# First layer's shift and scale summed by matmuls in four column groups, and split tiles read back through SyncE's queue

## The chip, the cores and the metric

One core of one Trainium2 chip (trn2). The metric is the device time of one execution in microseconds (us), lower is better. The engines are named as in the profile: PE (TensorE matmuls), PEld (its weight loads), DVE (VectorE), ACT (ScalarE), POOL (GpSimd), SP (SyncE, which here only issues DMAs).

## The reference

Two layers over x of 2048 tokens by 1024 features, one batch. Cut to what matters here:

```python
cond = jax.nn.silu(c)                                # 1024 numbers
for layer in range(2):
    mod = cond @ ada_w[layer] + ada_b[layer]         # 1024 x 3072 matrix, one row times matrix
    shift, scale, gate = jnp.split(mod, 3, axis=-1)
    h = x * (1.0 + scale) + shift
    if layer == 0:
        y = even_mixer(h)   # h @ w_in (1024 x 2816) -> windowed attention, gMLP gating, SiLU gate, @ w_out
    else:
        y = odd_mixer(h)    # h @ w_in (1024 x 2048) -> conv, gates (8 heads of 128 x 128), two scans, @ w_out
    x = layer_norm(alpha * x + gate * y)
```

All is float32. Every large product is made of three matmuls on operands that are split into a high and a low part: a is ahi + alo, b is bhi + blo, and the product is ahi*bhi + ahi*blo + alo*bhi.

## The kernel before

**The start (to about 55 us).** `modulation(...)` is called four times for layer 0, for shift and scale (`part` 0 and 1) of each half `n` of the features. Each call loads two tiles `aw` (1 MB each, [128, 4, 512], L166) through SP into a ring of three, and DVE adds up over the eight slices k in `macc`: L171 multiplies slice 0 by `cond[:, 0]`, L173 multiplies and adds the seven others. The 128 partition rows of `macc` are then summed on PE by four matmuls with a column of ones (L193), which also turn the result into a column, and DVE adds the bias (L198, L200). `build(u)` (L305-327) loads x (`xp`), transposes it on PE (L316), applies scale and shift on ACT (`hm`, L320), splits it into `hhi` and `hlo` (L148 on ACT, L149 on DVE) and stores both to `h_d` in DRAM. `split_w` (L475) loads eight tiles `raw` of the first weights and splits them into `wqh` (ACT, L148) and `wql` (DVE, L149). In code this goes half by half: shift and scale of n, build and split_w of n, then `project(blk)` runs the first products (L152 to L154 with `wqh`, `wql`, `hhi`, `hlo`).

**Even layer.** Attention runs block by block (scores L414, `P` shuffled by DMAs at L450, values L460). `load_hT` (L507-516) then reads `ahi`/`alo` of chunk t back from `h_d` with 8 DMAs on POOL's queue (L512, L513), and 12 to 40 weight units per chunk come as `raw` over SP and are split into the ring `hl` (8 buffers). Beside it, `prepare` splits all weights of the odd layer and stores them to `w_d` (40 tiles) and `wo_d` (16 tiles) of 512 KB.

**Odd layer (from about 890 us).** Four chunks t of 512 tokens and two halves s: `x_job` and `g_job` take 8 `hl` tiles each half and kind, loaded by `unit1` (L866) from `w_d` through POOL's queue; every tile serves 12 matmuls. `front` takes one `hg` tile per group of 128 features (L938, ring of 2) for the gate products `pm`, then ACT and DVE do gates and scans (L976 to L1010), POOL copies carries (L985, L990, L995) and adds the two directions (L996). `back` stores y (L1019, `y_d<-T`) and the carry weights (L1021, `b_d<-ii`) through SP. At the end `unit_out` (L1043) and `resident` (L1060) read `wo_d` on POOL's queue, and the tail reads `y_d` and `b_d` back on SP.

**What sets the order.** A scheduler with a model of the engines puts the instructions of each engine in one list ahead of time; each engine, and each queue of DMA issues, works its list off in that order. An instruction that waits holds up all behind it on its engine. A DMA tile in DRAM is float32; the split tiles in SBUF are float32r, the same 32 bits. Before, POOL's DMAs are given the two types as they stand.

Of the kernel before, what the change touches and what calls it, by code (L numbers as in the profile page):

```python
# [7 lines left out]
F32 = mybir.dt.float32  # L8
F32R = mybir.dt.float32r
I32 = mybir.dt.int32  # L10
AF = mybir.ActivationFunctionType
# [7 lines left out]
KD = D // 128  # L19
# [34 lines left out]
def kernel(  # L54
# [27 lines left out]
    nc = tc.nc  # L82
    act = nc.scalar.activation
# [19 lines left out]
    h_d = []  # L103
# [11 lines left out]
    wo_d = []  # L115
# [3 lines left out]
    w_d = []  # L119
# [8 lines left out]
    cond = const.tile([128, KD], F32, name="cond")  # L128
# [27 lines left out]
    def bank(p, tag, shape=(128, C)):  # L156
        t = p.tile(list(shape), F32, tag=tag, name=tag)
        return t

    def modulation(mp, pp, tag, layer, part, n, gate=None):  # L160
        c0 = part * D + n * C
        acc = mp.tile([128, C], F32, tag="macc", bufs=2, name="macc")
        m = mp.m
        for k2 in range(KD // m):
            aw = mp.tile([128, m, C], F32, tag=tag, name="aw")
            load(out=aw, in_=ada_w[layer, k2 * m * 128:(k2 + 1) * m * 128, c0:c0 + C].rearrange(  # L166
                "(j p) n -> p j n", p=128))
            for j in range(m):
                k = m * k2 + j
                if k == 0:  # L170
                    ts(out=acc, in0=aw[:, j], scalar1=cond[:, 0:1], scalar2=None, op0=ALU.mult)  # L171
                else:
                    stt(out=acc, in0=aw[:, j], scalar=cond[:, k:k + 1], in1=acc, op0=ALU.mult, op1=ALU.add)  # L173
        ps = bank(*pp)
        if part == 2:
            brow = mp.tile([1, C], F32, tag="brow", bufs=1, name="brow")
            load(out=brow, in_=ada_b[layer:layer + 1, c0:c0 + C])
            tt(out=acc[0:1, :], in0=acc[0:1, :], in1=brow, op=ALU.add)
            nc.tensor.matmul(ps, lhsT=ones, rhs=acc, start=True, stop=True)
            act(out=gate[:, n * C:n * C + C], in_=ps, func=AF.Copy)  # L180
            return
        if layer == 0:
            pr, ks = slice(0, 128), slice(4 * n, 4 * n + 4)
            parts = acc.rearrange("p (k m) -> p k m", k=4)
        else:
            pr, ks = slice(64 * n, 64 * n + 64), slice(0, 8)
            parts = mp.tile([128, 8, 64], F32, tag="parts", bufs=1, name="parts")
            for a in range(2):
                nc.vector.tensor_copy(parts[:, :, 32 * a:32 * a + 32],
                                      acc[:, 256 * a:256 * a + 256].rearrange("p (k q) -> p k q", k=8))  # L190
        w = ks.stop - ks.start
        for k in range(w):
            nc.tensor.matmul(ps[pr, k:k + 1], lhsT=parts[:, k], rhs=ones[:, 0:1], start=True, stop=True)  # L193
        dst = (shift, scale)[part][pr, layer, ks]
        v0 = layer * 24 + part * 8
        bias = vcol0[pr, v0 + ks.start:v0 + ks.stop]
        if part == 1:
            stt(out=dst, in0=ps[pr, 0:w], scalar=1.0, in1=bias, op0=ALU.add, op1=ALU.add)  # L198
        else:
            tt(out=dst, in0=ps[pr, 0:w], in1=bias, op=ALU.add)  # L200
# [4 lines left out]
    ap = pool(sb, "attn", right)  # L205
    ss = ExitStack()
    st = pool(ss, "setup", right)
# [26 lines left out]
    ps = bank(px, "px")  # L234
    nc.tensor.transpose(ps[:, 0:8], crow, ident[0:8, 0:8])
    act(out=cond, in_=ps[:, 0:8], func=AF.Silu)

    class Ring:
        def __init__(self, p, q, tag, bufs, m):
# [238 lines left out]
    wqh = jp.tile([128, KD, 768], F32R, name="wqh")  # L478
    wql = jp.tile([128, KD, 768], F32R, name="wql")
    for n in range(2):  # L480
        modulation(Ring(ap, st, "P", 3, 4), (psc, "psc"), "aw", 0, 0, n)
        modulation(Ring(ap, st, "P", 3, 4), (psc, "psc"), "aw", 0, 1, n)
        build(0, range(2 * n, 2 * n + 2))
        split_w(range(4 * n, 4 * n + 4))
        build(1, range(2 * n, 2 * n + 2))
# [22 lines left out]
    def load_hT(t):  # L508
        hT = ([], [])
        for k2 in range(4):  # L510
            hi, lo = act_pair()
            nc.gpsimd.dma_start(out=hi, in_=h_d[t][0][:, 2 * k2:2 * k2 + 2, :])  # L512
            nc.gpsimd.dma_start(out=lo, in_=h_d[t][1][:, 2 * k2:2 * k2 + 2, :])  # L513
            for j in range(2):
                hT[0].append(hi[:, j])
                hT[1].append(lo[:, j])
        return hT
# [345 lines left out]

    def unit1(i):
        hl = cp.tile([128, 2, C], F32R, tag="hl", bufs=8, name="hl")
        nc.gpsimd.dma_start(out=hl, in_=w_d[i])  # L866
        return hl

    def job1(hT, c0):
# [46 lines left out]
    def front(t, s, X):  # L916
# [4 lines left out]
        for g0 in range(0, 4, BATCH):  # L921
# [3 lines left out]
            for i in range(g0, g0 + BATCH):  # L925
# [9 lines left out]
                xlo = el("xlo", 2, F32R)  # L935
                split(xhi[:, w], xlo[:, w], xc[:, w])
                hl = rp.tile([128, 2, C], F32R, tag="hg", bufs=2, name="hg")
                nc.gpsimd.dma_start(out=hl, in_=w_d[32 + g])  # L938
                ra[i] = el2("ra", NEL)
                T[i] = el2("T", NEL)  # L940
                ii[i] = el2("ii", NEL)
# [98 lines left out]

    def unit_out(i):
        hl = cp.tile([128, 2, C], F32R, tag="hl", bufs=8, name="hl")
        nc.gpsimd.dma_start(out=hl, in_=wo_d[i])  # L1043
        return hl

    def part_out(ps, hl, k):
# [10 lines left out]

    def resident(p, n, k):
        w = p.tile([128, 2, C], F32R, name=f"wo{n}_{k}")
        nc.gpsimd.dma_start(out=w, in_=wo_d[n * KD + k])  # L1060
        wo[n][k] = w

    oq = pool(ctx, "outq", left)
# [126 lines left out]
```

## Time and profile before

| | |
|---|---|
| median of 3 runs | 1597.9 us (1594.98, 1597.9, 1599.78) |
| profiled execution, own time | 1601.77 us |
| its span, first to last instruction | 1600.0 us |
| mean granted TensorE clock | 0.977 |
| PE busy | 1481.9 us, 93 % |
| DVE / ACT / POOL busy | 1241.8 / 780.8 / 514.5 us |
| DMA | 366.73 MB, mean 229 GB/s |

The profile is of one execution: busy time is what an engine's instructions took, idle time is put down to what ended it. PE's instructions overlap in the pipeline, so a matmul that lasts 0.39 us lets the next one start after 0.23 us: the step from start to start in a timeline is what one of a row of matmuls costs.

### The profile page before, as it was taken

The numbers are of one execution on the slowest core, as the hardware profiler recorded it, in microseconds if no ns is written. First come the engines' busy times: TensorE is split into PE (matmuls) and PEld (weight loads), VectorE is DVE, ScalarE is ACT, GpSimd is POOL, SyncE is SP. The second block draws the span as 40 slices with busy tenths as digits, with TensorE's granted clock in tenths as the row PEclk, the third lists the DMA queues.
The fourth block names the chain that finished last, engine by engine and source line by source line (L and its number), as shares of the span: only waits on it lengthen the run. The fifth ranks groups of instructions, "written<-read, shape, count | busy, mean of one in ns | idle before, by whom it ended". The sixth has DMA issues, their size and how long they took to land. (4 is left out here: it accounts for less than half of the span.)

```text
span 1600.0 us, 21817 instructions
## 1 busy us (share of the span) xinstructions
PE 1481.9 (93%) x7032; PEld 1189.1 (74%) x7032; DVE 1241.8 (78%) x2243; ACT 780.8 (49%) x1454; POOL 514.5 (32%) x703
## 2 busy tenths in 40 slices
PE   3999999989999999999999879999899899979997
PEld 3887777757788777878877668777777778867886
DVE  8589888754689668857966756989979989887785
ACT  3577777542433432333334128388389588761100
POOL 1023222111004002200211445768657765423121
PEclk9899999999999999999999999999999999989999
DMA  9366776848899898988765698786797677569652
GB/s 341 120 171 202 208 214 190 251 129 293 251 309 278 256 280 290 334 255 266 260 232 165 191 236 212 230 203 223 241 213 225 189 227 234 169 212 367 218 198 85
DMA packets 204603, 366.73 MB, mean 229 GB/s; under 512 B 54568, under 2 KB 100804, under 8 KB 204488
## 3 DMA queue, kind: packets, MB, share of 16 engines
q1 hardware_dynamic: 166632, 235.25, 47.8%
q0 software_dynamic: 37856, 130.08, 26.9%
q8 instruction: 56, 0.92, 0.2%
q14 instruction: 59, 0.48, 0.1%
HBM read 264.07 MB, written 79.68 MB: 215 GB/s over the span
## 5 line engine op out<-in xcount | busy, mean ns | idle before, releaser
L148 ACT ACTIVATE hl<-raw 128x512 fp32r<-128x512 f32 x192 | 118.4, 627 | 197.9 <-DMA raw<-in_ev_w_in_dram 122.3
L152 PE MATMUL pj<-ahi,hl 128*128 128x512 f32 x512 | 201.5, 397 | 11.1 <-DMA hl<-w_d 10.0
L153 PE MATMUL pj<-alo,hl 128*128 128x512 f32 x512 | 201.8, 394 | 0.0
L154 PE MATMUL pj<-ahi,hl 128*128 128x512 f32 x512 | 201.2, 394 | 0.0
L149 DVE TENSOR_TENSOR hl<-raw,hl 128x512 fp32r<-128x512 f32 x192 | 132.1, 697 | 70.4 <-ACT hl L148 70.0
L152 PEld LDWEIGHTS pj<-ahi,hl 128*128 128x128 f32 x512 | 97.4, 190 | 35.3 <-DMA hl<-w_d 12.9
L154 PEld LDWEIGHTS pj<-ahi,hl 128*128 128x128 f32 x512 | 97.3, 190 | 20.9
L153 PEld LDWEIGHTS pj<-alo,hl 128*128 128x128 f32 x512 | 97.5, 190 | 20.4
L866 POOL DMA_DIRECT2D hl<-w_d x128 | 70.6, 554 | 77.8 <-PE pj L154 64.7
L148 ACT ACTIVATE phl<-praw 128x512 fp32r<-128x512 f32 x56 | 35.4, 632 | 122.1 <-DMA praw<-in_od_w_in_dram 63.7
L450 POOL DMA_DIRECT2D P<-T x88 | 49.6, 571 | 135.5 <-DVE T L443 96.5
L512 POOL DMA_DIRECT2D ahi<-h_d x16 | 8.8, 551 | 255.4 <-PE px L154 142.6
L415 DVE CUSTOM_DVE_ANT_0 P<-psc,mask,nsink 128x384 f32<-128x384 f32 (+1 forms) x128 | 73.7, 596 | 20.6 <-PE psc L414 20.0
L154 PE MATMUL pj<-wqh,hlo 128*128 128x512 f32 (+1 forms) x256 | 85.0, 346 | 3.7 <-DVE hlo L149 3.7
L152 PE MATMUL pj<-wqh,hhi 128*128 128x256 f32 (+1 forms) x256 | 88.1, 347 | 0.0
L153 PE MATMUL pj<-wql,hhi 128*128 128x256 f32 (+1 forms) x256 | 87.9, 343 | 0.0
L418 ACT ACTIVATE P<-P,nm 128x384 f32<-128x384 f32 (+1 forms) x128 | 76.8, 604 | 22.6 <-DVE nm L415 20.9
L148 ACT ACTIVATE ahi<-yt 128x512 fp32r<-128x512 f32 (+1 forms) x44 | 32.4, 745 | 107.5 <-DVE yt L1086 68.6
L144 POOL TENSOR_SCALAR rstd<-mv 128x1 f32<-128x1 f32 x32 | 24.5, 764 | 186.9 <-DVE mv L601 163.7
L762 POOL TENSOR_TENSOR alo<-hm,ahi 128x512 fp32r<-128x512 f32 x32 | 47.4, 1486 | 97.4 <-PE pja L154 65.5
L152 PE MATMUL pm<-xhi,hg 128*128 128x512 f32 (+3 forms) x160 | 57.5, 372 | 22.7 <-ACT ra L951 13.9
L932 DVE SCALAR_TENSOR_TENSOR xc<-X,vcol,xc 128x512 f32<-128x512 f32 (+2 forms) x96 | 77.8, 834 | 0.3
(297 smaller groups left out, 4502.9 us busy)
## 6 DMA issues: line engine op xcount, KB each, us to landing
hl<-w_d POOLq DMA_DIRECT2D x128, 512.0 KB, 5.3
raw<-in_ev_w_in_dram SPq DMA_DIRECT2D x128, 256.0 KB, 4.0
w_d<-phl SPq DMA_DIRECT2D x40, 512.0 KB, 4.3
aw<-in_ada_w_dram SPq DMA_DIRECT2D x32, 512.0 KB, 5.9
hg<-w_d POOLq DMA_DIRECT2D x32, 512.0 KB, 4.8
P<-T SPq DMA_DIRECT2D x128, 96.0 KB, 4.1
aw<-in_ada_w_dram SPq DMA_DIRECT2D x8, 1024.0 KB, 8.5
xp<-in_x_dram SPq DMA_DIRECT2D x32, 256.0 KB, 3.5
```

The lines of the kernel that those rows point to most:

```text
L144: nc.gpsimd.tensor_scalar(out=dst, in0=src, scalar1=mul, scalar2=EPS, op0=ALU.mult, op1=ALU.add)
L148: act(out=hi, in_=src, func=AF.Copy)
L149: tt(out=lo, in0=src, in1=hi.bitcast(F32), op=ALU.subtract)
L152: nc.tensor.matmul(ps, lhsT=ahi, rhs=bhi, start=first, stop=False)
L153: nc.tensor.matmul(ps, lhsT=ahi, rhs=blo, start=False, stop=False)
L154: nc.tensor.matmul(ps, lhsT=alo, rhs=bhi, start=False, stop=last)
L415: nc.vector.tensor_tensor_reduce(out=p[:, g, 0:W], in0=ps[:, 0:W], in1=mask[:, m0:m0 + W], scale=-0.125, scalar=nsink[:, h:h + 1], op0=ALU ...
L418: act(out=p[:, g, 0:W], in_=p[:, g, 0:W], func=AF.Exp, scale=-1.0, bias=nm[:, h:h + 1], accum_out=rs[:, h:h + 1])
L450: dma.dma_start(out=pv[32 * r:32 * r + 32, 0:nb, i], in_=T[32 * i:32 * i + 32, 0:nk].rearrange("p (j r) m -> p r j m", r=4)[:, r])
L762: nc.gpsimd.tensor_tensor(out=lo[:, j], in0=h, in1=hi[:, j].bitcast(F32), op=ALU.subtract)
L866: nc.gpsimd.dma_start(out=hl, in_=w_d[i])
L932: stt(out=xc[:, w], in0=xt[:, j0 + j:j0 + j + W], scalar=vcol1[:, 8 * j + g:8 * j + g + 1], in1=xc[:, w], op0=ALU.mult, op1=ALU.add)
```

## The change

Two parts. First, for layer 0, a tile `wide` [128, 8, 32] holds `cond` of slice k in column 0 of block k and zeros elsewhere. Each of the eight slices of `aw` becomes one f32 matmul with 32 weight columns and 512 moving columns, which writes partitions 32*(k % 4) and on of one PSUM bank; slices k and k + 4 add up in place. So one row of each group of 32 partitions holds a partial sum, the others zeros. ACT copies the bank to `macc`, and the rest of `modulation` (the four matmuls with ones, the bias) stays as it was. Layer 1 and the gates keep the sums on DVE.

Second, five kinds of loads of split tiles (32 of `load_hT`, 128 of `unit1`, 32 `hg`, 16 of `unit_out` and 16 of `resident`) go from POOL's queue to SP's, with the destination named as float32, so that the DMA is a copy of the same type.

```diff
-    def modulation(mp, pp, tag, layer, part, n, gate=None):
+    def modulation(mp, pp, tag, layer, part, n, gate=None, wide=None):
...
+        sums = None if wide is None else bank(*pp)
...
-                if k == 0:
+                if sums is not None:
+                    q = 32 * (k % 4)
+                    nc.tensor.matmul(sums[q:q + 32, :], lhsT=wide[:, k], rhs=aw[:, j], start=k < 4, stop=k >= 4)
+                elif k == 0:
                     ts(out=acc, in0=aw[:, j], scalar1=cond[:, 0:1], scalar2=None, op0=ALU.mult)
                 else:
                     stt(out=acc, in0=aw[:, j], scalar=cond[:, k:k + 1], in1=acc, op0=ALU.mult, op1=ALU.add)
+        if sums is not None:
+            act(out=acc, in_=sums, func=AF.Copy)
...
+    wide = st.tile([128, KD, 32], F32, name="wide")
+    nc.gpsimd.memset(wide, 0.0)
+    nc.vector.tensor_copy(wide[:, :, 0], cond)
...
-        modulation(Ring(ap, st, "P", 3, 4), (psc, "psc"), "aw", 0, 0, n)
-        modulation(Ring(ap, st, "P", 3, 4), (psc, "psc"), "aw", 0, 1, n)
+        modulation(Ring(ap, st, "P", 3, 4), (psc, "psc"), "aw", 0, 0, n, wide=wide)
+        modulation(Ring(ap, st, "P", 3, 4), (psc, "psc"), "aw", 0, 1, n, wide=wide)
...
-            nc.gpsimd.dma_start(out=hi, in_=h_d[t][0][:, 2 * k2:2 * k2 + 2, :])
-            nc.gpsimd.dma_start(out=lo, in_=h_d[t][1][:, 2 * k2:2 * k2 + 2, :])
+            nc.sync.dma_start(out=hi.bitcast(F32), in_=h_d[t][0][:, 2 * k2:2 * k2 + 2, :])
+            nc.sync.dma_start(out=lo.bitcast(F32), in_=h_d[t][1][:, 2 * k2:2 * k2 + 2, :])
...
-        nc.gpsimd.dma_start(out=hl, in_=w_d[i])
+        nc.sync.dma_start(out=hl.bitcast(F32), in_=w_d[i])
...
-                nc.gpsimd.dma_start(out=hl, in_=w_d[32 + g])
+                nc.sync.dma_start(out=hl.bitcast(F32), in_=w_d[32 + g])
...
-        nc.gpsimd.dma_start(out=hl, in_=wo_d[i])
+        nc.sync.dma_start(out=hl.bitcast(F32), in_=wo_d[i])
...
-        nc.gpsimd.dma_start(out=w, in_=wo_d[n * KD + k])
+        nc.sync.dma_start(out=w.bitcast(F32), in_=wo_d[n * KD + k])
```

The order of the lists moves with it at three places. DVE in the start, before, from the scale of the first half on (`macc` is the sum of one call):

```order
L198 SCALAR_TENSOR_TENSOR scale_139<-psc_285,vcol0_136 128x4
L171 TENSOR_SCALAR macc_371<-aw_372,cond_135 128x512
L173 SCALAR_TENSOR_TENSOR macc_371<-aw_372,cond_135,macc_371 128x512
L149 TENSOR_TENSOR wql_252<-raw_335,wqh_251 128x768
L173 SCALAR_TENSOR_TENSOR macc_371<-aw_372,cond_135,macc_371 128x512 x2
L149 TENSOR_TENSOR hlo_294<-hm_300,hhi_293 128x512
L149 TENSOR_TENSOR hlo_310<-hm_316,hhi_309 128x512
L173 SCALAR_TENSOR_TENSOR macc_371<-aw_378,cond_135,macc_371 128x512 x3
L149 TENSOR_TENSOR hlo_342<-hm_348,hhi_341 128x512
L173 SCALAR_TENSOR_TENSOR macc_371<-aw_378,cond_135,macc_371 128x512
```

The same stretch of DVE's list after the change:

```order
L206 TENSOR_TENSOR shift_138<-psc_271,vcol0_136 128x4
L204 SCALAR_TENSOR_TENSOR scale_139<-psc_292,vcol0_136 128x4
L149 TENSOR_TENSOR wql_255<-raw_338,wqh_254 128x768
L149 TENSOR_TENSOR hlo_301<-hm_307,hhi_300 128x512
L149 TENSOR_TENSOR hlo_317<-hm_323,hhi_316 128x512
L149 TENSOR_TENSOR wql_255<-raw_342,wqh_254 128x768
L206 TENSOR_TENSOR shift_138<-psc_393,vcol0_136 128x4
L149 TENSOR_TENSOR hlo_349<-hm_355,hhi_348 128x512
L149 TENSOR_TENSOR wql_255<-raw_452,wqh_254 128x768
```

DVE keeps the splits and the bias; the sums between them are gone from its list.

PE at the very start, before:

```order
L193 MATMUL psc_266<-ones_133,macc_253 128x1 x4
L282 MATMUL px_239<-ident_131,vrow0_176 128x56
L316 MATMUL px_295<-ident_131,xp_291 128x128 x4
L316 MATMUL px_311<-ident_131,xp_307 128x128 x4
L193 MATMUL psc_285<-ones_133,macc_272 128x1 x4
L316 MATMUL px_343<-ident_131,xp_339 128x128 x4
L316 MATMUL px_359<-ident_131,xp_355 128x128 x4
L152 MATMUL pj_493<-wqh_251,hhi_293 128x256
L153 MATMUL pj_493<-wql_252,hhi_293 128x256
```

and after (`psc` takes the sums, `32x512` is one of the column groups):

```order
L173 MATMUL psc_257<-aw_258,wide_188 32x512 x4
L173 MATMUL psc_257<-aw_264,wide_188 32x512 x4
L199 MATMUL psc_271<-ones_133,macc_256 128x1 x4
L173 MATMUL psc_278<-aw_279,wide_188 32x512 x4
L291 MATMUL px_242<-ident_131,vrow0_176 128x56
L325 MATMUL px_302<-ident_131,xp_298 128x128 x4
L325 MATMUL px_318<-ident_131,xp_314 128x128 x4
L173 MATMUL psc_278<-aw_285,wide_188 32x512 x4
L199 MATMUL psc_292<-ones_133,macc_277 128x1 x4
L173 MATMUL psc_379<-aw_380,wide_188 32x512 x4
L173 MATMUL psc_379<-aw_386,wide_188 32x512 x4
L152 MATMUL pj_504<-wqh_254,hhi_300 128x256
```

The sums of three calls stand ahead of the first product of the first projection; those of the fourth stand between its products.

POOL's list in the odd layer, before, where it issues the tiles `w_d28` to `w_d30` of the second half of chunk 1 (`hg` is a tile of the gates, `T`, `ii` are the scans' results):

```order
L996 TENSOR_TENSOR T_10254<-T_10254 128x512
L938 DMA hg_10807<-w_d36_127 128x1024
L985 COPY carry_f_143<-T_10291 128x1
L990 COPY first_h_146<-T_10291 128x1
L995 COPY first_a_147<-ii_10255 128x1
L996 TENSOR_TENSOR T_10291<-T_10291 128x512
L866 DMA hl_11054<-w_d28_119 128x1024
L995 COPY first_a_147<-ii_10292 128x1
L938 DMA hg_10844<-w_d37_128 128x1024
L866 DMA hl_11068<-w_d29_120 128x1024
L866 DMA hl_11082<-w_d30_121 128x1024
```

SP's list after, with the same tiles:

```order
L947 DMA hg_10397<-w_d35_126 128x1024
L1028 DMA y_d_73<-T_9875 128x510
L875 DMA hl_11009<-w_d24_115 128x1024
L1028 DMA y_d_73<-T_9912 128x510
L1030 DMA b_d_74<-ii_9876 128x510
L1030 DMA b_d_74<-ii_9913 128x510
L875 DMA hl_11023<-w_d25_116 128x1024
L875 DMA hl_11037<-w_d26_117 128x1024
L875 DMA hl_11051<-w_d27_118 128x1024
L875 DMA hl_11065<-w_d28_119 128x1024
L947 DMA hg_10818<-w_d36_127 128x1024
L875 DMA hl_11079<-w_d29_120 128x1024
```

The loads stood behind POOL's copies and adds of the scans; now they stand behind the stores of y and of the carry weights.

## Rows read from the trace of the kernel before

**Rows 1.** Section 1 and two rows of section 2 of the page: busy time of each engine, and the span in 40 slices of 40 us (busy tenths of PE; granted TensorE clock in tenths).

```profile
PE 1481.9 (93%) x7032; PEld 1189.1 (74%) x7032; DVE 1241.8 (78%) x2243; ACT 780.8 (49%) x1454; POOL 514.5 (32%) x703
...
PE   3999999989999999999999879999899899979997
...
PEclk9899999999999999999999999999999999989999
```

**Rows 2.** Waits of PE over the whole span: engine, line and tile, what it waited for, us in total, times, longest us.

```profile
PE psc L193 <- DVE macc L173: 15.7, 3, 9.7
...
PE pj L152 <- DMA hl<-w_d: 10.0, 7, 2.9
...
PE pm L152 <- DMA hg<-w_d: 5.2, 3, 2.6
...
PE pja L152 <- DMA ahi<-h_d: 1.8, 1, 1.8
```

**Rows 3.** Busy time of each engine in stretches of 4 us of the start, with the granted clock, the DMA share and the rate: the columns are us, PE, PEld, DVE, ACT and POOL busy (instructions), PEclk, DMA share, GB/s.

```profile
8.00:12.00 4.00, 0.00 (x0) 0.00 (x0) 4.00 (x10) 0.00 (x0) 0.00 (x0) 1.00 1.04 313
36.00:40.00 4.00, 0.17 (x2) 0.09 (x1) 3.89 (x7) 0.00 (x0) 0.00 (x0) 0.79 1.03 351
40.00:44.00 4.00, 1.75 (x8) 1.38 (x8) 3.14 (x5) 0.00 (x0) 0.00 (x0) 0.50 1.07 392
44.00:48.00 4.00, 2.51 (x11) 2.05 (x12) 1.14 (x3) 3.32 (x7) 0.00 (x0) 0.50 0.39 140
```

**Rows 4.** The costliest group of DVE's instructions from 0 to 56 us: count, busy us, mean ns of one, idle before.

```profile
L173 DVE SCALAR_TENSOR_TENSOR macc<-aw,cond,macc 128x512 f32<-128x512 f32 x28 | 20.9, 746 | 0.4
```

**Rows 5.** Timeline of DVE from 36 to 46 us: start us, us, engine, line, instruction, count, idle before and its releaser.

```profile
37.30 0.47 DVE L171 TENSOR_SCALAR macc<-aw,cond 128x512 f32<-128x512 f32 x1
37.81 5.47 DVE L173 SCALAR_TENSOR_TENSOR macc<-aw,cond,macc 128x512 f32<-128x512 f32 x7
45.24 0.16 DVE L198 SCALAR_TENSOR_TENSOR scale<-psc,vcol 128x4 f32<-128x4 f32 x1 [1.96 <-PE psc L193]
```

**Rows 6.** Timeline of PE from 40 to 50 us (columns as in the group above).

```profile
43.34 1.86 PE L193 MATMUL psc<-ones,macc 128*128 128x1 f32 x8 [0.41 <-DVE macc L173]
...
48.91 0.42 PE L153 MATMUL pj<-wql,hhi 128*128 128x256 f32 x1
49.12 0.63 PE L152 MATMUL pj<-wqh,hhi 128*128 128x512 f32 x1
49.55 0.63 PE L153 MATMUL pj<-wql,hhi 128*128 128x512 f32 x1
```

**Rows 7.** Timeline of SP, the DMA queue's own, from 28 to 43 us: two of its issues.

```profile
30.73 0.57 SPq L166 DMA_DIRECT2D aw<-in_ada_w_dram  x1
...
41.23 0.34 SPq L475 DMA_DIRECT2D raw<-in_ev_w_in_dram  x1
```

**Rows 8.** DMA issues from 0 to 56 us: count, KB each, median us from issue to landing.

```profile
raw<-in_ev_w_in_dram SPq DMA_DIRECT2D x8, 384.0 KB, 5.6
```

**Rows 9.** Timeline of PE from 200 to 206 us: the values matmuls of one attention block, 64 columns each, in the two column halves by turns.

```profile
203.69 2.79 PE L460 MATMUL po<-P,vt 128*64 128x512 f32 x12
```

**Rows 10.** Line 179 (the gate's f32 matmul over 128 columns, x8): duration of one in ns, min/median/max, first and last start, shape.

```profile
L179 PE MATMUL pm<-macc,ones x8: 590/591/667, 425.9 to 590.3; 128*128 128x512 f32 x8
```

**Rows 11.** Groups of ACT's instructions from 0 to 56 us by line and shape: a copy of one bank of 512 columns.

```profile
L347 ACT ACTIVATE qk<-pj 128x512 f32<-128x512 f32 x1 | 0.6, 598 | 0.5 <-PE pj L154 0.5
```

**Rows 12.** Timeline of PE from 1120 to 1130 us: two of its waits for a split tile.

```profile
1124.92 0.50 PE L152 MATMUL pj<-ahi,hl 128*128 128x512 f32 x1 [1.73 <-DMA hl<-w_d]
...
1128.78 0.79 PE L152 MATMUL pj<-ahi,hl 128*128 128x512 f32 x1 [2.89 <-DMA hl<-w_d]
```

**Rows 13.** Timeline of POOL from 1105 to 1126 us.

```profile
1107.16 1.06 POOL L866 DMA_DIRECT2D hl<-w_d  x2
1111.84 1.04 POOL L985 COPY carry_f<-T 128x1 f32<-128x1 f32 x1 [3.62 <-DVE T L981]
...
1114.02 2.06 POOL L996 TENSOR_TENSOR T<-T 128x512 f32<-128x512 f32 x1
...
1119.35 2.13 POOL L996 TENSOR_TENSOR T<-T 128x512 f32<-128x512 f32 x1
1121.42 0.57 POOL L866 DMA_DIRECT2D hl<-w_d  x1
...
1123.46 1.07 POOL L866 DMA_DIRECT2D hl<-w_d  x2
```

**Rows 14.** Waits of SP's DMA queue from 1000 to 1400 us, the largest: line, what it waited for, us in total, times, longest us.

```profile
SPq L1019 <- DVE T L1010: 297.5, 23, 43.2
```

**Rows 15.** Sections 3 and 6 of the page: DMA queues with packets, MB and share of 16 engines; issues with count, KB each, median us from issue to landing.

```profile
q1 hardware_dynamic: 166632, 235.25, 47.8%
q0 software_dynamic: 37856, 130.08, 26.9%
...
hl<-w_d POOLq DMA_DIRECT2D x128, 512.0 KB, 5.3
...
hg<-w_d POOLq DMA_DIRECT2D x32, 512.0 KB, 4.8
```

**Rows 16.** Section 5 of the page, two groups of POOL's DMA issues: busy us, mean ns of one, idle before and what ended most of it.

```profile
L866 POOL DMA_DIRECT2D hl<-w_d x128 | 70.6, 554 | 77.8 <-PE pj L154 64.7
...
L512 POOL DMA_DIRECT2D ahi<-h_d x16 | 8.8, 551 | 255.4 <-PE px L154 142.6
```

## Prediction

> **What bounds the kernel now.** I read the page first: PE is busy 1481.9 of 1600.0 us, in nearly all slices after the first at nine tenths and at full clock [rows 1]. So a microsecond comes back only where PE stands idle, and the next view is PE's waits [rows 2]. The reader is to see three entries that the change touches: 15.7 us for the sums in `macc` at the start, 10.0 + 5.2 = 15.2 us for `hl` and `hg` tiles in the odd layer, and 1.8 us for `ahi` tiles. Together 32.7 us, 2 % of the span, is all that the change can remove directly. What follows is how much of it is given to another wait. About 0.3 % (4.8 us) is what a measurement of this kernel can tell from no change.
>
> **The start: what goes.** The stretches of 4 us [rows 3] show two limits side by side. From 8 to 12 us and from 36 to 44 us the DMA share stands at 1.03 to 1.07: the transfers fill the start until 44 us, when the last weights are on their way. In the same time DVE does 28 sums of 746 ns, 20.9 us, and four shorter ones ahead of them [rows 4, 5]. The last call is the plain case: its first sum starts at 37.30, the seven others take 5.47 us, PE's L193 runs at 43.34, and the scale is there at 45.24 [rows 5, 6]. Steady products on PE begin at 48.91 [rows 6], and they begin with slice 4 of the first projection, since slices 4 to 7 need that scale.
>
> All of that goes, but I do not count it, because the transfers cover most of it. I count two things. (a) The same tiles must land. At the rate of 40 to 44 us, 392 GB/s, the stretch from 8 to 12 us (313) is short by 0.32 MB and that from 36 to 40 us (351) by 0.16 MB, 1.2 us together. The last `raw` leaves at 41.23 [rows 7]; at the median of 5.6 us [rows 8] it lands near 47, and from 44 to 47 us the queues ran at 140 GB/s instead of 392, 0.75 MB or 1.9 us. So with full queues the last weights land about 3 us earlier. (b) The last `aw` leaves at 30.73 [rows 7], held by a ring whose slots DVE frees. In the changed list PE frees them and that load stands further ahead, and the chain behind it loses the seven sums. So the second half's scale should be there well before the last weights, and slices 4 to 6 need no longer wait for it. One slice is three matmuls of 256 columns and three of 512, at steps of 0.21 and 0.43 us at the half clock of that stretch [rows 3, 6]: 1.9 us, three slices 5.8 us. Full gain (a) + (b): 8.8 us.
>
> **The start: what is added.** 32 matmuls of 32 columns. The nearest row is the values matmuls with 64 columns, two groups by turns: 12 in 2.79 us, 0.47 us a pair [rows 9]; a full-width f32 matmul of 512 columns lasts 0.59 us alone [rows 10]. If four groups share the array as two do, eight waves cost 8 x 0.47 = 3.7 us, at the half clock 7.4; if no group runs beside another, 32 x 0.59 = 19 us, at the half clock 38. I take 4 to 7 us, since two groups already share in the trace. The cover is PE's 15.7 us at `macc`, which the sums themselves replace, so I price them at nothing; without sharing and at the half clock they would eat the gain and some 10 us more. Four copies of a bank on ACT, 0.6 us each [rows 11], lie in the chain of each call, as do the four L193 matmuls that stay; ACT waits for weights in this stretch, so it has the room. The clock is at half from 40 to 48 us after PE idled [rows 3]; sums on PE there may keep it up, which I do not count.
>
> For the start I take -6, between 3 and 8.8, and keep -9 and +4 as ends: the range for copies and sums that land in the wrong order on PE, which works its list off and has three calls' sums ahead of the first product.
>
> **The odd layer: what goes.** PE waits 1.73 and 2.89 us for `hl` tiles at 1124.92 and 1128.78 [rows 12]. POOL shows why [rows 13]: after two loads at 1107.16 it stands 3.62 us for a scan, copies carries, adds two directions in 2.06 and 2.13 us, and issues the next `hl` at 1121.42 and 1123.46. In 14 us PE eats five tiles (12 matmuls at a step of 0.23 us, 2.8 us a tile). So the tile was late because of what stood ahead on POOL, not because of the transfer. Ten such gaps make the 15.2 us [rows 2]. On SP none of that work stands ahead: -15.2 is the end on one side.
>
> **The odd layer: what comes.** SP's list has its own waiting instructions: 23 waits of the y stores for DVE, 297.5 us in all and 43.2 at the longest [rows 14]. Nothing that matters is queued behind them now; after the change the next `hl` and `hg` are. The cover: `hl` has a ring of 8, 8 x 2.8 = 22 us of PE work less a landing of 5.3 [rows 15], 17 us; `hg` has two buffers only and a landing of 4.8, so its cover is the thin one. The stores come in six lots (three chunks, two halves). If each lot costs one new gap of the kind now seen, 15.2 / 10 = 1.5 us at the mean and 2.9 at the longest, the price is 9 to 17 us, and the net between -6 and +2. I take -4, since the scheduler has the loads spread between the stores, with most of them asked for well ahead.
>
> In return a load that waits for PE to free its buffer now holds up a y store behind it. The stores are read only at the end of the kernel, so I give this nothing but the tiles `T` that they free late.
>
> **The rest, at nothing.** The queues: 235.25 MB on the hardware queue take 47.8 % and 130.08 MB on the software queue 26.9 % [rows 15], 0.20 and 0.21 % a MB, so a byte costs the same on either. POOL loses 224 issues at 537 to 554 ns, over 120 us, as `hl`'s 70.6 us show [rows 16], but PE's list of waits has no large entry for it [rows 2]. `load_hT` stands 255.4 us at the head of POOL's queue, mostly for PE [rows 16]; on SP weight loads stand behind such a wait, with 8 `hl` buffers as cover. I price it at 0, with ends of -2 (the 1.8 us of `ahi`) and +5.
>
> The Trainium skill speaks against the second part: its page "DMA: Bandwidth & Descriptors", section "Issuing engines are not separate DMA queues", says that issuing from several engines only saves the time on the sequencer that an issue takes, usually little beside the DMA itself. By that alone the moved loads are worth nothing, and the sum would be -6. The rows of POOL disagree in that the issue was late by other work on the engine, which the page's sentence does not weigh.
>
> **The sum.** -6 at the start, -4 in the odd layer, 0 elsewhere: -10. Against the profiled execution of 1601.77 us (span 1600.0) that is 1591.8; it ran 3.9 us above the median of 1597.9, so on the scale of the runs 1587.9, say 1588. The ends of the terms are -9 - 15 = -24 (1574) and +4 + 2 + 5 = +11 (1609).
>
> **Rivals.**
> 1. Both gains nearly full, SP's stores hurting nowhere: -14 to -24, 1574 to 1584. For it: 17 us of cover on `hl`. Against: `hg` with two buffers, and a wait of 43.2 us. 12 in 100.
> 2. The moved loads change nothing in sum, each gap on POOL replaced by one on SP (the result that the page's sentence also gives): the start alone, -3 to -6, about 1593. 24 in 100, half of it within 0.3 %.
> 3. The first part does not do what it says: the transfers hold the start where it is, or the groups run one after the other, and only the odd layer gives 0 to 4: about 1596. 10 in 100.
> 4. Slower: `hg` or `hl` stands behind a y store until it is already needed. Then each costs a full landing, 5.3 us. It decides from (15.2 + 6 + 4.8) / 5.3, about five such places; with all six lots it is 32 - 15 - 6 = +11, 1609. For it: 297.5 us of waits on that queue. Against: a ring of eight, loads spread between the stores. 14 in 100, 11 of them beyond 0.3 %.
>
> **How the numbers follow.** The forecast has 40 in 100, -7 to -13. Faster by over 0.3 %: 40 + 12 + 12 = 64; within: 12 + 10 + 3 = 25; slower: 11. The range from 1576 to 1602 leaves out the lower half of rival 1 and the part of rival 4 beyond 0.3 %, 17 in 100.
>
> **What would show it.** At the start: no L173 sums on DVE, PE's wait at `macc` gone, waves of four `psc` matmuls with a step of some 0.12 us, steady products from 40 to 46 us with slices 4 to 6 done before the last weights. In the odd layer: no gap of `hl` at the places of [rows 12], and each new gap of `hg` or `hl` just behind a y or carry store in SP's timeline. I am wrong if PE's waits for `hl` and `hg` come to more than 15 us, if steady products begin as late as now, or if a wait appears in the even layer behind `load_hT`.

## The result and the profile after

| | before | changed |
|---|---|---|
| median (4 runs each, same chip) | 1597.47 us | 1583.13 us |
| lowest to highest | 1594.98 to 1599.78 | 1581.08 to 1584.51 |
| span of the profiled execution | 1600.0 us | 1582.8 us |

The ratio is 0.9902, with an interval of 0.988 to 0.9925: 14.3 us faster. The forecast was 10 us, 1588, in a range of 1576 to 1602. A second measurement on another chip (below) gave 0.9905, 0.9885 to 0.9924.

The page of the changed kernel, section 1, section 3 and two rows of section 6. It answers to [rows 1, 15].

```profile
PE 1491.3 (94%) x7096; PEld 1186.1 (75%) x7096; DVE 1218.3 (77%) x2212; ACT 782.8 (49%) x1458; POOL 416.8 (26%) x480
...
q1 hardware_dynamic: 198888, 352.71, 69.2%
q0 software_dynamic: 5600, 12.62, 3.1%
...
hl<-w_d SPq DMA_DIRECT2D x128, 512.0 KB, 4.6
...
hg<-w_d SPq DMA_DIRECT2D x32, 512.0 KB, 4.3
```

DVE has 23.5 us less to do, POOL 97.7 less, PE 9.4 more. PE has 64 records more for 32 matmuls: an f32 matmul is two records (a record is one entry of the trace).

The waits of PE in the changed kernel, columns as in [rows 2].

```profile
PE pm L153 <- DVE xlo L149: 9.8, 7, 3.0
PE pm L152 <- ACT ra L960: 7.5, 5, 2.3
PE psc L173 <- DMA aw<-in_ada_w_dram: 5.6, 3, 3.1
PE pj L152 <- ACT ahi L148: 4.5, 1, 4.5
PE po L469 <- DMA P<-T: 4.2, 1, 4.2
PE pj L152 <- ACT G L912: 3.9, 1, 3.9
...
PE pja L152 <- DMA ahi<-h_d: 2.8, 1, 2.8
...
PE psc L199 <- ACT macc L179: 2.2, 3, 0.8
...
PE pm L152 <- DMA hg<-w_d: 2.0, 1, 2.0
```

Of the 15.2 us for `hl` and `hg` in [rows 2], 2.0 are left; of the 15.7 us for `macc`, 2.2, and 5.6 for `aw` have come. PE's wait for `xlo`, the split that DVE makes ahead of the gates, has grown from 1.7 to 9.8 us, that for `P` from 1.4 to 4.2, that for `ahi` from 1.8 to 2.8; 3.9 for `G`, which ACT makes, is new. The wait for `ra` has shrunk from 13.9 to 7.5.

The wait for `hg` that is left, on SP's queue and on PE:

```profile
1139.14 0.34 SPq L1028 DMA_DIRECT2D y_d<-T  x1
...
1139.57 0.38 SPq L947 DMA_DIRECT2D hg<-w_d  x1
...
1144.31 0.47 PE L152 MATMUL pm<-xhi,hg 128*128 128x512 f32 x1 [1.96 <-DMA hg<-w_d]
```

The `hg` load leaves just behind a y store that had waited 1.4 us for DVE.

The start, in stretches of 4 us (columns as in [rows 3]) and then PE's timeline from 19 to 45 us.

```profile
36.00:40.00 4.00, 3.26 (x23) 1.80 (x21) 2.26 (x3) 2.43 (x4) 0.00 (x0) 1.00 1.07 377
40.00:44.00 4.00, 1.76 (x10) 1.34 (x11) 1.64 (x3) 3.27 (x8) 0.00 (x0) 0.80 1.00 348
44.00:48.00 4.00, 4.00 (x14) 3.39 (x13) 2.65 (x4) 1.54 (x2) 0.00 (x0) 0.50 1.05 378
```

```profile
19.86 1.93 PE L173 MATMUL psc<-aw,wide 128*32 128x512 f32 x8
...
23.55 1.06 PE L173 MATMUL psc<-aw,wide 128*32 128x512 f32 x8
...
43.50 0.58 PE L152 MATMUL pj<-wqh,hhi 128*128 128x256 f32 x1 [1.89 <-ACT hhi L148]
```

From 44 to 48 us 378 GB/s flow, where 140 did [rows 3], and the first product of slice 4 starts at 43.50. Before, it stood 5.1 us later:

```profile
48.55 0.56 PE L152 MATMUL pj<-wqh,hhi 128*128 128x256 f32 x1
```

The weights did not come 3 us earlier, though. The last `raw` leaves at 41.36 us, where it left at 41.23 [rows 7], and ACT splits it at 46.16, 1.7 us earlier than before (47.83). The granted clock from 40 to 48 us is 0.80 and 0.50. A wave of four matmuls, eight records, takes 1.06 us or 1.93.

Where the time came from is best read from three milestones that every kernel here has: the last values matmul of attention, the last product of the even layer, and the first and last product of the odd layer's projection. They are the last start in the rows `po<-T`, `pjb<-hl,ahi` and `pj<-ahi,hl` of each trace; of the changed kernel they read:

```profile
L469 PE MATMUL po<-T,vt x20: 592/593/643, 330.1 to 345.6; 128*64 128x512 f32 x20
```

```profile
L152 PE MATMUL pj<-ahi,hl x512: 387/389/795, 903.5 to 1366.9; 128*128 128x512 f32 x171
...
L153 PE MATMUL pjb<-hl,ahi x128: 387/389/628, 423.1 to 903.1; 128*128 128x512 f32 x128
```

| profiled execution | attention ends | even layer ends | even layer takes | odd projection takes | rest of the span | span |
|---|---|---|---|---|---|---|
| before | 347.6 | 908.3 | 560.7 | 476.6 | 214.7 | 1600.0 |
| before, once more | 348.6 | 905.5 | 556.9 | 473.5 | 215.5 | 1595.0 |
| sums only | 342.6 | 896.8 | 554.2 | 470.7 | 214.4 | 1582.4 |
| loads only | 350.7 | 911.4 | 560.7 | 467.5 | 215.2 | 1594.6 |
| loads without load_hT | 347.9 | 904.4 | 556.5 | 467.5 | 215.6 | 1587.9 |
| changed | 345.6 | 903.1 | 557.5 | 463.4 | 215.9 | 1582.8 |
| changed, once more | 345.0 | 902.3 | 557.3 | 463.4 | 215.3 | 1581.4 |
| changed, load_hT on POOL | 343.6 | 904.9 | 561.3 | 469.6 | 217.0 | 1592.0 |
| the same, once more | 341.0 | 894.8 | 553.8 | 466.7 | 216.8 | 1578.8 |
| second half's sums only | 344.6 | 911.6 | 567.0 | 469.4 | 215.4 | 1596.9 |
| the same, load_hT on POOL | 344.3 | 901.9 | 557.6 | 463.3 | 216.1 | 1581.8 |
| one column group | 363.8 | 922.2 | 558.4 | 464.0 | 215.3 | 1601.9 |

The odd projection's stretch is its last start less its first, the rest of the span what follows. Two executions of the kernel before differ by 5 us, and two of the kernel with `load_hT` on POOL, on two chips, by 13.2, of which 7.5 lie in the even layer. So single differences of some us in this table prove nothing, and the even layer's column does not tell the kernels apart. Two columns do, each by a narrow gap. Attention ends at 341.0 to 345.6 us in the seven profiles with sums in four groups, and at 347.6 to 350.7 in the four with all sums on DVE. The odd projection takes 463.3 to 469.6 us in the nine with `unit1`'s loads on SP, and 470.7 to 476.6 in the three of this table with them on POOL.

### The profile page after: what moved, and what is told of

Its sections match the earlier page's. It is cut to its first block, busy times and chain, and to the rows that moved or that the text cites. A ratio compares the mean times of both kernels' runs of the same rounds, so it can differ in the third digit from the quotient of the medians.

```text
span 1582.8 us, 21904 instructions
## 1 busy us (share of the span) xinstructions
PE 1491.3 (94%) x7096; PEld 1186.1 (75%) x7096; DVE 1218.3 (77%) x2212; ACT 782.8 (49%) x1458; POOL 416.8 (26%) x480
## 4 chain that ended last, share of the span: by engine, by line
PE 48%; DVE 19%; DMA 15%; ACT 8%; issue 5%; SPq 3%; POOL 1%; DVEq 0%; POOLq 0%; ACTq 0%
PE pj L152 8%; PE pj L153 8%; PE pj L154 8%; DMA raw<-in_ev_w_in_dram 3%; DMA praw<-in_od_w_in_dram 3%; PE po L469 3%; DVE hl L149 2%; PE pm L152 2%; DVE xc L941 2%; PE pm L153 2%; PE pm L154 2%; DMA raw<-in_ev_w_out_dram 2%; DMA praw<-in_od_w_out_dram 2%; ACT ra L976 1%; PE px L154 1%
## 5 line engine op out<-in xcount | busy, mean ns | idle before, releaser
L144 POOL TENSOR_SCALAR rstd<-mv 128x1 f32<-128x1 f32 x32 | 30.9, 964 | 473.3 <-DVE mv L610 362.6
L424 DVE CUSTOM_DVE_ANT_0 P<-psc,mask,nsink 128x384 f32<-128x384 f32 (+1 forms) x128 | 73.8, 596 | 23.5 <-PE psc L423 23.4
L1005 POOL TENSOR_TENSOR T<-T 128x512 f32<-128x512 f32 (+2 forms) x32 | 60.4, 1889 | 79.2 <-DVE T L996 42.9
L941 DVE SCALAR_TENSOR_TENSOR xc<-X,vcol,xc 128x512 f32<-128x512 f32 (+2 forms) x96 | 74.0, 794 | 0.2
L971 DVE SCALAR_TENSOR_TENSOR ii<-ii,xc 128x1024 f32<-128x1024 f32 (+2 forms) x32 | 42.7, 1334 | 37.9 <-ACT ii L965 37.9
L152 PE MATMUL pm<-xhi,hg 128*128 128x512 f32 (+3 forms) x160 | 56.8, 370 | 14.3 <-ACT ra L960 7.5
```

The lines of the kernel that those rows point to most:

```text
L152: nc.tensor.matmul(ps, lhsT=ahi, rhs=bhi, start=first, stop=False)
L424: nc.vector.tensor_tensor_reduce(out=p[:, g, 0:W], in0=ps[:, 0:W], in1=mask[:, m0:m0 + W], scale=-0.125, scalar=nsink[:, h:h + 1], op0=ALU ...
L941: stt(out=xc[:, w], in0=xt[:, j0 + j:j0 + j + W], scalar=vcol1[:, 8 * j + g:8 * j + g + 1], in1=xc[:, w], op0=ALU.mult, op1=ALU.add)
L1005: nc.gpsimd.tensor_tensor(out=T[i][:, 0, w], in0=T[i][:, 0, w], in1=T[i][:, 1, w], op=ALU.add)
```

## The experiments

All ratios are to the kernel before on the same chip. The first four ran on one chip.

**The sums alone.** The changed kernel with this put back (and the like for the four other loads):

```diff
-        nc.sync.dma_start(out=hl.bitcast(F32), in_=w_d[i])
+        nc.gpsimd.dma_start(out=hl, in_=w_d[i])
```

> The changed kernel with its loads of split tiles back on POOL's queue: the first part alone. By the prediction the start gives -6 against the kernel before, so about 1591. The lead of the changed kernel over the one before, read product by product, says less: 5.1 us at the first slice that needs the second scale, but 2 us by 54 us. If that lead is the start's, the time is -2 to -5, 1593 to 1596. The stretch from 940 to 980 us, where the changed kernel gains 11 us, should show no gain here by either theory.

Measured 1586.53 us against 1599.99, ratio 0.9909 (0.9884 to 0.9933): 13.5 us, more than either expectation. Attention ends 5 us earlier than before, but not all of that is the start's. The 64 transposes of `ks` stand in attention from its beginning to near its end; their row gives the first and the last start. Before, with the sums alone, and with the second half's sums alone (a run below):

```profile
L370 PE MATMUL px<-ident_r,ks x64: 222/228/305, 58.4 to 283.7; 128*128 128x128 f32 x64
```

```profile
L379 PE MATMUL px<-ident_r,ks x64: 221/227/306, 56.6 to 278.0; 128*128 128x128 f32 x64
```

```profile
L379 PE MATMUL px<-ident_r,ks x64: 222/227/306, 54.2 to 278.5; 128*128 128x128 f32 x64
```

With the sums alone PE is 1.8 us ahead at the first and 5.7 at the last, so some 4 us arose inside attention. One wait of PE there, from 62 to 280 us, differs by nearly as much: the one for `hlo`, which DVE splits. Again before, the sums alone, the second half alone:

```profile
PE pj L154 <- DVE hlo L149: 3.7, 3, 2.2
```

```profile
PE pj L154 <- DVE hlo L149: 0.2, 1, 0.2
```

```profile
PE pj L154 <- DVE hlo L149: 3.1, 4, 2.2
```

All waits of PE in that stretch come, in the profiles of the table above, to 6.4 or 6.5 us in the four with all sums on DVE, to 2.9 to 3.9 in the five with all of them in four groups, and to 5.7 or 5.8 in the two with the first half on DVE. This speaks for DVE's freed time, but not alone: with one column group, where DVE has none of these sums either, they are 7.2. The rest of the 13.5 us arose after attention, and against the expectation part of it between 940 and 980 us: PE's wait there is 3.81 us instead of 8.65.

**The loads alone.** The kernel before with the opposite edit on all five kinds of loads.

> The kernel before with the five kinds of loads on SP's queue: the second part alone. By the prediction (T1: loads late behind POOL's own work) -4 and the gaps for hl and hg tiles gone, 1593. By the rival (T2: one queue in place of two; the pieces of x_d for chunk 1, xp, land after 21 us at the worst beside hl transfers of the other queue, and DVE stands 14.5 us at their first transpose) -9 to -13, 1585 to 1588, with DVE's wait for xp under 5 us and most of the gain between 940 and 980 us.

Measured 1597.11, ratio 0.9976 (0.996 to 0.9993): 2.9 us, near the forecast's 4 and far from T2's 9 to 13, although T2's sign came: DVE's longest wait for `xp` is 3.4 us. The table shows a sum of two larger parts: attention ends 2.1 to 3.1 us later than in the two profiles of before, the odd projection takes 6 to 9 us less.

**The loads on ACT.** As the loads alone, with `nc.scalar.dma_start`.

> The kernel before with the five kinds of loads issued by ACT instead of POOL, as plain copies. T1 asks only that POOL's work no longer stands ahead, but ACT's own work now does: 1590 to 1600. T2 asks whether hl and xp share one queue: ACT's issues are another ring than SP's, so xp still shares the engines with hl, DVE's wait for xp stays above 8 us and the stretch from 940 to 980 us gains little.

Measured 1614.25, ratio 1.0079 (1.0053 to 1.0106): slower, beyond T1's range. PE waits longer for two things that ACT makes:

```profile
PE pm L152 <- ACT ra L951: 16.0, 7, 5.5
...
PE pm L152 <- ACT xhi L148: 8.2, 4, 3.7
```

Before, these were 13.9 and 2.9 us. But the profile loses 6.3 us by the end of attention, 4.9 in the even layer and 5.6 in the odd projection, so these two are not the whole. That ACT's work is late behind the loads it issues, T1's mechanism in reverse, fits this and is not shown by it. DVE's longest wait for `xp` was 5.9 us, below the 8 that T2 asked for, with ACT's loads on a hardware queue of their own (117.45 MB, beside 235.25 on SP's): two queues do not by themselves bring back the long waits for `xp`.

**xp on POOL.** The kernel before with `nc.gpsimd.dma_start` for the four pieces of `xp` in `build1`.

> The kernel before with the loads of xp for the odd layer moved from SP's queue to POOL's, so that they stand in one queue with hl. T1: POOL's list gets 64 more issues of some 0.55 us, loads are later, no gain or a loss of up to 5 us. T2: xp no longer shares the engines with transfers that were asked for later; DVE's wait for xp at chunk 1 falls under 6 us from 14.5, and the time by 5 to 10 us.

Measured 1634.67, ratio 1.0205 (1.0176 to 1.0234): 35 us slower. The place itself did what T2 says, PE's wait fell from 8.65 to 1.15 us; DVE's longest wait for `xp` fell to 8.0, not under 6. But POOL's queue then stood 23.0 us in nine waits at `xp` for DVE, with the loads of `hl` behind it, and in this profile the odd projection takes 485.8 us. What follows it takes 237.7 instead of 214.7, for which I have no reason. As a test of the time it says nothing for T2; what a waiting load ahead costs a queue it shows only in part.

**The kernel before, once more.**

> The kernel before, unchanged, profiled once more. With the first part alone the lists from the end of attention on are the same row by row as before, and yet 11 of the 17 us between the two profiles arise there: 2.6 and 1.6 us at two waits for yt in the even layer, and 4.8 us at 958 us, where PE waits 8.65 us before and 3.81 us with the sums, behind DVE's wait for xp. If those places are chance (when a transfer lands), this profile has other gaps there than 8.65 and 2.58 us. If they follow from DVE being ahead after the sums, the same gaps stand here again, within half a microsecond.

One run, 1596.72 us. The timeline of PE at the place in question, and DVE's waits for `xp` from 900 to 1200 us:

```profile
952.81 0.79 PE L152 MATMUL pm<-xhi,hg 128*128 128x510 f32 x1 [6.38 <-ACT ra L951]
953.40 0.63 PE L153 MATMUL pm<-xlo,hg 128*128 128x510 f32 x1
953.83 0.63 PE L154 MATMUL pm<-xhi,hg 128*128 128x510 f32 x1
...
956.46 0.46 PE L154 MATMUL pj<-ahi,hl 128*128 128x512 f32 x1
956.76 0.39 PE L152 MATMUL pm<-xhi,hg 128*128 128x510 f32 x1
956.99 0.39 PE L153 MATMUL pm<-xlo,hg 128*128 128x510 f32 x1
```

```profile
DVE hm L759 <- DMA xp<-x_d: 12.6, 2, 11.5
```

6.38 us instead of 8.65, and no wait of 2.58 us for `yt`: part of what the first two profiles showed there was chance. The longer wait for `xp` is not. In the three profiles with the loads on POOL and `xp` on SP, DVE's longest wait for `xp` in the odd layer was 14.5, 11.5 and 8.3 us (before, before again, sums alone); in the nine with both on SP it was 3.0 to 4.9.

**One column group.** The changed kernel with all eight slices summed in one group:

```diff
-                    q = 32 * (k % 4)
-                    nc.tensor.matmul(sums[q:q + 32, :], lhsT=wide[:, k], rhs=aw[:, j], start=k < 4, stop=k >= 4)
+                    nc.tensor.matmul(sums[0:32, :], lhsT=wide[:, k], rhs=aw[:, j], start=k == 0, stop=k == KD - 1)
```

> The changed kernel with all eight slices of a call summed in one column group of 32 (and the copy and the last sum cut to these 32 partitions). If four groups share the array, a wave of four takes longer here: in the changed kernel it takes 1.0 us at full clock and 1.87 at half. By the steps of two halves in attention (0.2325 us a record, two records a matmul) a wave without sharing is 4 x 2 x 0.2325 = 1.86 us at full clock and 3.7 at half, so 8 waves take 7 to 12 us more of PE. My forecast says these are covered by PE's idle time, of which 14.6 us is left in the start: 0 to 5 us slower than the changed kernel. If nothing covers them, 7 to 12 us slower.

Measured 1603.62, ratio 1.0015 (0.9998 to 1.0032): the whole gain of the change is gone, some 18 us beside the changed kernel's ratio, against 7 to 12 at most in the expectation. The group of the sums from 0 to 62 us, of this kernel and of the changed one (first profile):

```profile
L172 PE MATMUL psc<-aw,wide 128*32 128x512 f32 x64 | 33.0, 673 | 3.1 <-DMA aw<-in_ada_w_dram 3.1
```

```profile
L173 PE MATMUL psc<-aw,wide 128*32 128x512 f32 x64 | 12.9, 889 | 5.7 <-DMA aw<-in_ada_w_dram 5.6
```

The columns are busy us, mean ns of one, and idle before. The same 64 records take 20.1 us more of PE without the four groups, although each is shorter on average: the records of different groups overlap. At a granted clock of 1.00 (the stretches 44 to 48 us here and 36 to 40 above) eight records take, in one group and in four:

```profile
44.92 3.62 PE L172 MATMUL psc<-aw,wide 128*32 128x512 f32 x8
```

```profile
37.14 1.07 PE L173 MATMUL psc<-aw,wide 128*32 128x512 f32 x8
```

The Trainium skill, page "TensorEngine Tiling (Array Packing)", section "Theoretical Speedup", gives up to 4 times for 32 columns; here it is 33.0 / 12.9 = 2.6 over the whole start, and 3.4 for these two waves. Some 18 of the added 20 us show in the time, so little covered them. That the sums in four groups had used the cover up already is not shown.

**The second half alone.** The changed kernel with `wide=wide if n == 1 else None`.

> The changed kernel with shift and scale of the first half of the features summed on DVE as before, and only those of the second half on TensorE. By the prediction it is the scale of the second half that holds the first products of the second slices, so nearly the whole gain stays: within 2 us of the changed kernel. If it is DVE's work that counts, wherever it stands in the start, half of the gain of the first part (some 6 us) is lost.

Measured 1590.59, ratio 0.9935 (0.9912 to 0.9958): against the first half of the expectation, some 5 us of the changed kernel's gain are lost, by ratios from two chips whose intervals overlap (the changed kernel's is 0.988 to 0.9925). The sums took 4.9 us of PE and the granted clock stayed at 1.00 until 60 us, so the start itself was good: the first transpose of `ks` stands 4.2 us ahead of before, more than in any other profile. At the last the lead is 5.2, and PE waits 3.1 us for `hlo` again (the rows above). That fits the second half of the expectation, DVE's work, and is no proof of it.

**load_hT back on POOL.** The changed kernel with the two lines of `load_hT` as before.

> The changed kernel with the 32 loads of ahi and alo (load_hT) back on POOL's queue, all other loads on SP. In the profiles the loads alone cost 6 to 12 us between 290 and 560 us, in the even layer, and win more than that in the odd one. If load_hT on SP's queue, ahead of the weight loads, is that cost, this kernel is 4 to 8 us faster than the changed one, 1575 to 1579. If the cost comes from elsewhere in the even layer, it is within 2 us of it.

Measured 1577.6, ratio 0.9859 (0.9833 to 0.9885). It came to the expected gain, but on another chip than the changed kernel, so the next four ran side by side.

> The changed kernel, unchanged, beside the three others on one chip, so that they can be compared with it directly: a ratio of 0.988 to 0.9925 to the kernel before, as measured first. In its profile the sums take 12.9 us of PE again, and PE has no gap of over 5 us between 930 and 980 us; if one stands there, the 11 us won there in the first profile were partly chance.

> The changed kernel with the loads of load_hT on POOL's queue, once more and beside the changed kernel itself. If load_hT on SP holds up the weight loads of the even layer, it is 4 to 8 us faster than the changed kernel on the same chip; if the 1577.6 us of the run before came from the chip or from chance, within 2 us of it.

> As the run before, and the first half's shift and scale summed on DVE. In the profile of the second half alone PE took 4.9 us for the sums instead of 12.9, kept full clock until 60 us and stood 6.1 us ahead of the kernel before at its 48th product, against 2.2 us for the changed kernel; but by the middle of attention both stood 4 to 6 us ahead, and its time was 7 us above the changed kernel's. If the start decides, 0 to 4 us faster than the run before, 1574 to 1578. If it is DVE's work that counts, some 6 us slower, 1583.

> The kernel before with all loads of split tiles on SP but those of load_hT. With load_hT the loads alone gave 2.9 us: a loss of about 6 in the even layer and a gain in the odd one. Without it, if load_hT was the loss, -8 to -12 us, 1588 to 1592; the sums' -13.5 us and this together would then make the -22 us of the kernel with both. If not, -3 us again.

| | median | ratio | interval |
|---|---|---|---|
| before | 1602.83 | | |
| changed | 1587.31 | 0.9905 | 0.9885 to 0.9924 |
| changed, load_hT on POOL | 1580.91 | 0.9865 | 0.9848 to 0.9882 |
| the same, first half's sums on DVE | 1584.49 | 0.988 | 0.986 to 0.9899 |
| loads alone, without load_hT | 1590.59 | 0.9922 | 0.99 to 0.9944 |

The changed kernel came out as expected: in its profile the sums take 12.0 us, and PE has no gap over 0.3 us between 930 and 980 us. With the first half's sums on DVE the time is 1584.49, where the expectation has it if DVE's work counts (1583) and not if the start decides (1574 to 1578), but its interval overlaps that of the run beside it. The loads without `load_hT` fell in the 1588 to 1592 that holds if `load_hT` was the loss.

So `load_hT` on SP's queue costs 6.4 us beside the sums and some 9 without them (0.9976 against 0.9922, on two chips), twice with the same sign. The kernel with `load_hT` on POOL is faster than both given ones; its interval and that of the changed kernel do not overlap on this chip, by a narrow margin (0.9882 and 0.9885). DVE's waits from 280 to 900 us for the `aw` tiles of layer 1's shift and scale and of the gates show where it falls, first of the changed kernel (once more), then of the one with `load_hT` on POOL:

```profile
DVE macc L177 <- DMA aw<-in_ada_w_dram: 23.4, 5, 9.0
```

```profile
DVE macc L177 <- DMA aw<-in_ada_w_dram: 11.0, 7, 3.6
```

In the five profiles of the table above with `load_hT` on SP this wait is 20.5 to 24.9 us, in the seven with it on POOL 8.5 to 14.2. One place of it, the changed kernel once more and then the one with `load_hT` on POOL:

```profile
430.34 1.40 SPq L522 DMA_DIRECT2D alo<-h_d  x1
432.57 0.57 SPq L167 DMA_DIRECT2D aw<-in_ada_w_dram  x1
443.68 1.54 DVE L177 SCALAR_TENSOR_TENSOR macc<-aw,cond,macc 128x512 f32<-128x512 f32 x2 [8.98 <-DMA aw<-in_ada_w_dram]
```

```profile
431.75 0.38 SPq L167 DMA_DIRECT2D aw<-in_ada_w_dram  x1
436.31 1.54 DVE L177 SCALAR_TENSOR_TENSOR macc<-aw,cond,macc 128x512 f32<-128x512 f32 x2 [0.86 <-DMA aw<-in_ada_w_dram]
```

The `aw` load leaves only 0.8 us later behind four loads of `load_hT`, of which the last is shown; most of the 9 us is that it lands later.

The shuffles `P` of attention's last blocks stand on SP's queue too, but they are no cost in all: from 280 to 900 us PE waits 3.9 us for them in the first kernel and 4.6 in the second. How the 6 to 9 us reach PE is shown only in part. From 280 to 900 us PE waits 2.1 to 3.5 us for the splits `hl` in the five profiles and at most 1.0 in the seven, up to 3.3 for `ahi` instead of up to 2.2, and for what comes of `macc` no longer than before.

## Why the prediction came out right

The sum was right in sign and within its range, but its split was not: two terms were too small and one that I set to nothing was a loss. That -10 lies near -14.3 is in part luck: the sums gave 13.5 us where I had 6, the loads without `load_hT` 12.2 where I had 4, and `load_hT` took 6 to 9 back. With its 14.3 us the result lies outside the -7 to -13 of the forecast and at the near end of rival 1, both gains nearly full, to which I gave 12 in 100; its condition, that SP's stores hurt nowhere, held but for 2.0 us.

- **The start, -6: right in part.** Term (b) came, slice 4 starts 5.1 us earlier. Term (a) did not: the queues are full after 44 us, but the last weights are split 1.7 us earlier and not 3. And the lead doesn't last as I summed it: at the changed kernel's first transpose of `ks` (56.4 us against 58.4) 2.0 us of it are left. The 5.0 us at the end of attention (6.0 against the second profile of before) come near -6 only because some 4 us arise inside attention.
- **The price of the sums, 4 to 7 us: mis-sized.** They took 12.9 us (12.0 in the second profile). I read a row of 12 records as 12 matmuls; they are 6, as the 64 records for 32 matmuls show. The same reading gave 19 us for no sharing, where one group took 33.0. Pricing them at nothing was possible only with the four groups.
- **What the sums give after the start: not forecast.** 13.5 us were measured for the sums alone, 5 to 6 of them by the end of attention. From there on the lists of PE and SP are those of the kernel before, row by row. The profile shows 2.7 to 6.5 us less in the even layer and 2.8 to 5.9 less in the odd one than the two profiles of before. With DVE's first half kept, some 4 to 5 us are lost in two runs, each with an interval that overlaps its neighbour's. For attention the wait is PE's for `hlo`, 3.7 us before and 0.2 with the sums. For what arises after attention no run shows the wait by which DVE's freed time would act; this part of the cause stays open.
- **The odd layer, -15.2 removed and 9 to 17 added: the mechanism was half right.** The gaps for `hl` and `hg` went, to 2.0 us, as in the term for what goes. The step that failed is where the new waits come from, and their price. The one gap that is left is of the kind I named, an `hg` load just behind a y store (the rows of SP above). It costs 2.0 us, where I had 9 to 17 for six lots of stores. On SP y stores now wait 8.4 us for DVE at the longest, 65.1 in all from 1000 to 1400 us, instead of 297.5 [rows 14]. The waits that grew are PE's for `xlo` and `G`, that is for DVE and ACT. And I missed the gap at 958 us: `xp` pieces stood on SP's queue and `hl` loads on POOL's, `xp` landed after up to 20.9 us, DVE stood, then ACT, then PE. With both on SP's queue the longest landing was 8.6 to 10.3 us. That the two queues' sharing of the DMA engines makes `xp` late is argued, not shown; with the loads on ACT's queue it was 12.6. The loads without `load_hT` gave 12.2 us (9 to 16) instead of 4.
- **load_hT at 0, with +5 as the end: the step that failed outright.** It costs 6 to 9 us, and the sign of being wrong that I gave, a wait in the even layer behind `load_hT`, came true. I named the wait for PE at the head of the queue and priced its followers at nothing, because `hl` has eight buffers. The follower that shows is `aw`, for which DVE waits 20.5 to 24.9 us instead of 8.5 to 14.2. The end of -2 for `ahi` did not come either: PE's wait for it grew from 1.8 to 2.8 us.
- **The rule that issuing engines are no separate queues** (the Trainium skill, "DMA: Bandwidth & Descriptors", "Issuing engines are not separate DMA queues") as a rival: by it the loads are worth nothing. The same loads gave 0.9976 from SP and 1.0079 from ACT on one chip, and 0.9922 from SP without `load_hT`. So the issuer alone moved the time by 16 us here, more than the rule gives. What waits ahead of a DMA and behind it on its issuer is the likelier reason; no run isolates it.

Rival 4, slower by stores ahead of tiles, showed in one place of 2.0 us; the condition of rival 3 is what the one-group run makes: with groups that don't run beside each other the gain is nil.

## What to carry to other kernels

Before loads move to another engine's queue, list the two or three loads that will stand just behind each one that can wait, and price those, not the moved ones; here 32 of 224 loads took back some 9 of the 12 us that the others gave. The row-times-matrix sums paid on TensorE here only in column groups that ran beside each other; count a matmul's records before a price is read from a row. And test the parts of a change one by one even if the whole is faster: the fastest kernel here has both parts but for 32 of the loads.

## What the runs showed of the hardware

This wait of PE cost more than its length. After the 6.38 us above, the eight matmuls from 952.81 to 956.76 start 0.3 to 0.8 us apart, mostly 0.43, and only from there on 0.23; the granted clock of that stretch, of the same trace:

```profile
948.00:952.00 4.00, 0.00 (x0) 0.00 (x0) 4.00 (x7) 2.96 (x4) 1.36 (x1) 0.72 0.82 147
952.00:956.00 4.00, 3.05 (x6) 2.00 (x7) 4.00 (x5) 2.88 (x6) 2.56 (x3) 0.50 0.20 34
956.00:960.00 4.00, 4.00 (x18) 3.23 (x17) 2.93 (x5) 4.00 (x8) 2.87 (x3) 0.93 0.92 221
```

From 952.81 to 956.76 the eight take 3.95 us, at 0.23 each they would take 1.84: the wait costs 2.1 us more than it lasts, most of it at the lower level of 1.2 GHz. Eight steps of 0.43 would be 3.4 us; the rest lies in longer steps, 0.77 at the most, which the lower level alone does not give. My sum took waits at their length.

The other surprise: in the changed kernel a wave of sums took 1.93 us at 19.86 and 1.06 at 23.55, with the granted clock of the stretches from 16 to 24 us at 1.00. The four L199 matmuls show the same step. The granted clock does not explain it, and I have no run that does. In the second profile of the changed kernel the first of these waves took 1.06 us already, which is the difference between the 12.9 us of sums and the 12.0.
